# Four modulation rows summed in other places, and a softmax with its sink among the scores

## Chip, cores and metric

One core of a Trainium2 chip. The metric is the device time of one execution in microseconds; lower is better. TensorE's clock has two levels, 1.2 and 2.4 GHz; the profile gives the granted share of the higher one.

## The reference, cut to what matters

One transformer layer on 1024 latent tokens of width 1024 with 256 context tokens: a modulated norm, eight heads of windowed attention beside a short convolution, an output projection, then a mixture of 16 experts.

```python
mod = silu(c) @ w_ada + b_ada                # (1024) @ (1024, 6*1024)
sh1, sc1, gt1, sh2, sc2, gt2 = split(mod, 6)
h = modulate(rmsnorm(x, g_mix), sh1, sc1)    # r*(1+scale)+shift
q, k, v, bg, cg, hv = split(h @ w_in)
att = windowed_attention(rope(q), rope(k), v, k_ctx, v_ctx, sink)
#   p = softmax([sink, q.k_ctx/8, q.k_loc/8]); the sink's share is dropped
conv = bg * conv3(cg * hv)
x = x + gt1 * (concat(att, conv) @ w_out)
h2 = modulate(rmsnorm(x, g_ffn), sh2, sc2)
x = x + gt2 * expert_choice_ffn(h2, w_router, w_gate, w_up, w_down)
return rmsnorm(x, g_final)
```

The text calls gt1, sh2, sc2 and gt2 the rows 0 to 3. `sh1` and `sc1` are computed first, on TensorE, and stay as they are.

## The kernel before

All products that need fp32 accuracy are made of three fp32r products: each operand is split into a rounded high part (ScalarE) and a low part, source minus high (VectorE or GpSimd).

The order of TensorE's instructions is as written. Those of the other engines, and of the SP queue that issues loads, are put in order by a planner from a time model, by readiness and priority; each engine then runs its own list in order. `weave` mixes streams: each stream yields weights, and the stream that has done the smallest share of its total goes on.

*Projections.* `kv_stream` runs over 24 steps: eight 128-column groups of the 256 context tokens, then of the first and of the second 512 latent tokens. A step calls `build_hT` (transposes on TensorE, scale and shift, high part, low part; even and odd groups on different engines, L290 to L298) and three steps later `proj_kv`. `q_stream` follows, one tile of 128 tokens after the other: 24 matmuls, rotation and split on VectorE and ScalarE (L506 to L511), then, inside the next tile, eight transposes (`q_turn`). It also turns the late keys. The key/value weights are split at L264 to L269, their low part on GpSimd.

Beside these runs `mod_stream`, woven from 18 of 56 parts on. For each of the rows 0 to 3 and each of eight 128-row groups of `w_ada` it loads 128x1024 numbers (L461), ScalarE multiplies them by silu(c) of the partition (L462) and GpSimd adds them to the row's accumulator (L464). TensorE sums each accumulator over the partitions by a selection matrix (L474), `b_ada` is added, and the four rows go to memory (`rows_d`).

*Attention and convolution* are woven next. A unit is a pair of heads of one 128-token tile, 32 in all. `scores` makes the scores in PSUM; VectorE adds the mask and takes the maximum with 8 times the sink (L576); L578 scales it to the exponential's bias; ScalarE takes the exponential and its sum (L579); L586 to L589 add exp(sink - maximum) to the sum and invert it. Both heads are then scaled, and `values` transposes, splits and multiplies them. The score buffers are two slots in turn. `conv` loads a weight block one part ahead (12 parts) and GpSimd makes its low part (L712). `router_consts` (L650) reads rows 1 and 2 back in transposed form.

*Output projection.* For each tile 48 matmuls (L879), the residual on VectorE (L884), the norm, and beside it routing and sorting of earlier tiles (L1001 to L1067), nearly all on VectorE. The split tokens `ah` rotate through three free slots. Experts' weights are prefetched into the other slots.

The last uses are: row 0 at L777, rows 1 and 2 at L831 to L835 and in `router_consts`, row 3 in the experts.

Of the kernel before, what the change touches and what calls it, by code (L numbers as in the profile page):

```python
# [86 lines left out]
def tile_layer(ctx, tc, x, c, cx, c_ctx, w_ada, b_ada, g_mix, w_in, conv_w, sink, w_out, g_ffn,  # L87
# [59 lines left out]
    nc.sync.dma_start(small[8:16], c_ctx.rearrange("(k p) -> k p", p=128))  # L147
    nc.sync.dma_start(small[16:32], b_ada[:, 0:2 * D].rearrange("o (k p) -> (o k) p", p=128))
    nc.sync.dma_start(small[32:40], g_mix.rearrange("o (k p) -> (o k) p", p=128))
    nc.sync.dma_start(small[40:52], conv_w.rearrange("o t (f p) -> (o t f) p", p=128))  # L150

# [15 lines left out]
    nc.vector.memset(ones_b, 1.0)  # L167
    sel = consts.tile([128, 4, 4], F32, name="sel")
    nc.vector.memset(sel, 0.0)
    for r in range(4):  # L170
        nc.vector.memset(sel[:, r, r:r + 1], 1.0)

    smallT = consts.tile([128, 52], F32, name="smallT")
    ps = p1n("ps_small")
    nc.tensor.transpose(ps[:, :52], small[:52], ident[:52, :52])
    nc.vector.tensor_copy(smallT, ps[:, :52])
    gmixT = smallT[:, 32:40]
    convT_w = smallT[:, 40:52]

# [96 lines left out]
    nc.sync.dma_start(sinkb, sink.partition_broadcast(128).rearrange("p o h -> p (o h)"))  # L276
    nc.vector.tensor_scalar(sink8, sinkb, 8.0, None, op0=OP.mult)

# [3 lines left out]
    def build_hT(tiles, j, hT, k, mem=None):  # L282

        n = 128 * len(tiles)
        ps = p1n("ps_xt", 3)
        for i, t in enumerate(tiles):
            nc.tensor.transpose(ps[:, i * 128:(i + 1) * 128], t[:, k * 128:(k + 1) * 128], ident)
        hf = mem[:, k % 4] if mem is not None else w4("hf", (n,), tag=("w4", "wm")[k % 2])
        hi, lo = hT[2 * (k // 4)][0][:, k % 4], hT[2 * (k // 4) + 1][0][:, k % 4]
        if k % 2:  # L290
            nc.scalar.activation(hf, ps[:, :n], AF.Identity, scale=mscale[:, k, j:j + 1], bias=mshift[:, k, j:j + 1])
            nc.vector.tensor_copy(hi, hf)
            nc.vector.tensor_tensor(lo, hf, hi.bitcast(F32), op=OP.subtract)
        else:
            nc.vector.tensor_scalar(hf, ps[:, :n], mscale[:, k, j:j + 1], mshift[:, k, j:j + 1],
                                    op0=OP.mult, op1=OP.add)
            nc.scalar.copy(hi, hf)
            (nc.gpsimd if mem is None or k < 4 else nc.vector).tensor_tensor(lo, hf, hi.bitcast(F32), op=OP.subtract)  # L298

# [154 lines left out]

    mrows = p2(0, "mrows")

    def mod_row(r, acc):

        for k in range(KC):
            wt = wm("wmod")  # L460
            nc.sync.dma_start(wt, wada_k[k][:, (2 + r) * D:(3 + r) * D])  # L461
            nc.scalar.activation(wt if k else acc, wt, AF.Copy, scale=silu_c[:, k:k + 1])  # L462
            if k:
                nc.gpsimd.tensor_tensor(acc, acc, wt, op=OP.add)  # L464
            yield 1

    def mod_stream():
        yield 18
        accs = []

        def sums(j):
            for r in (2 * j, 2 * j + 1):
                for n in range(2):
                    mm(mrows[:4, n], sel[:, r], accs[j][0][:, r % 2, n * 512:(n + 1) * 512], start=r == 0, stop=r == 3)  # L474
            slots.put(accs[j][1])

        for j in range(2):
            accs.append(slots.get((2, D), F32, "acc"))
            g = [mod_row(2 * j + i, accs[j][0][:, i]) for i in range(2)]
            for k in range(KC):  # L480
                for q in g:
                    yield next(q)
                if j == 1 and k == 2:
                    sums(0)
        bias = w4("bias")
        nc.sync.dma_start(bias[0:4], b_ada[:, 2 * D:6 * D].rearrange("o (r f) -> (o r) f", r=4))
        yield 3
        yield 3
        sums(1)
        nc.vector.tensor_tensor(bias[0:4], mrows[:4].rearrange("p a b -> p (a b)"), bias[0:4], op=OP.add)  # L490
        nc.sync.dma_start(rows_d, bias[0:4])

# [42 lines left out]

    weave([(urgent(steps(kv_stream(), q_stream())), 95.0), (mod_stream(), 56.0)])
    for r in wq:
# [14 lines left out]
    def scores(u):  # L552
# [4 lines left out]
        loc = slice(blocks[0] * 128, (blocks[-1] + 1) * 128)  # L557
        sm2, s_sm = slots.get((2, 640), F32, "sm")
        for i in range(2):
# [14 lines left out]
            else:  # L574
                mk = maskt[:, 0:W]
            nc.vector.tensor_tensor_reduce(dst, src, mk, op0=OP.add, op1=OP.max, scale=1.0,  # L576
                                           scalar=sink8[:, h:h + 1], accum_out=mx[:, b, h:h + 1])
# [7 lines left out]
        r = rec[:, b, hs]  # L585
# [14 lines left out]
    def values(u):  # L600
# [49 lines left out]
    def router_consts():  # L650
# [7 lines left out]
        nc.sync.dma_start(wr, w_router.rearrange("o (k p) e -> p (o k) e", p=128))  # L658
        modT = work.tile([24, 128], F32, tag="sa", name="modT")
        for i, src in enumerate((rows_d[1], rows_d[2], g_ffn[0])):  # L660
            nc.sync.dma_start(modT[8 * i:8 * i + 8], src.rearrange("(k p) -> k p", p=128))
        yield
        pmod = p1(2, "pmod")
        nc.tensor.transpose(pmod[:, :24], modT, ident[:24, :24])
        b2T = consts.tile([128, KC], F32, name="b2T")
        s2T = consts.tile([128, KC], F32, name="s2T")
        nc.vector.tensor_copy(s2T, pmod[:, 16:24])
        nc.vector.tensor_copy(b2T, pmod[:, 0:8])
        nc.vector.scalar_tensor_tensor(s2T, pmod[:, 8:16], 1.0, s2T, op0=OP.add, op1=OP.mult)
        yield  # L670
# [144 lines left out]

    weave([(steps(attention(), prepare()), 160.0), (conv(), 161.0)])

# [14 lines left out]
    bcast_row(S2, rows_d[2])  # L832
    gf = wm("gf")
    bcast_row(gf, g_ffn[0])
    nc.vector.scalar_tensor_tensor(S2, S2, 1.0, gf, op0=OP.add, op1=OP.mult)  # L835

# [308 lines left out]
    def beside(t, others):  # L1145
# [323 lines left out]
def _constants():  # L1469
# [10 lines left out]
    amask = np.zeros((128, 768), np.float32)  # L1480
    amask[:, 256:384] = np.where(j >= q, 0.0, NEG)
    amask[:, 512:640] = np.where(j <= q, 0.0, NEG)
    amask = amask.astype(ml_dtypes.bfloat16)
# [33 lines left out]
```

## Time and profile before

| | us |
|---|---|
| median of 3 runs (1166.91 to 1170.52) | 1169.38 |
| the profiled execution | 1168.05 |
| its span, first to last instruction | 1166.3 |
| TensorE busy | 1061.0 (91%) |
| VectorE busy | 966.0 (83%) |
| ScalarE busy | 765.4 (66%) |
| GpSimd busy | 353.3 (30%) |
| mean granted TensorE clock | 0.961 |

The span is what the trace covers; the rest of an execution lies around it. Busy shares are means over stages with different limits, so the rows below go by stretches. A busy TensorE may still run at half its clock, and the time of an instruction on VectorE or GpSimd includes the time in which it is held.

### The profile page before, as it was taken

The page shows a single profiled execution, that of the slowest core. Times are in us where ns is not written, and L with a number is a line of the kernel's source. Part 1 is how long each engine was busy: PE and PEld are TensorE (multiplying, and loading weights), DVE is VectorE, ACT ScalarE, POOL GpSimd, SP SyncE. Part 2 cuts the span into 40 slices and gives each one's busy share as a digit, 9 for nine tenths or more (in the row PEclk, how much of TensorE's full clock was granted, in tenths as well). Part 3 has the DMA queues.
Part 4 walks back from the last instruction along what each step waited for, and adds up shares of the span by engine and source line. Part 5 has one row for each costly group of instructions (what it writes and reads, how often), then busy time and mean ns, then how long its engine had stood idle before and what let it go on. Part 6 is the DMA issues. An engine that isn't in the chain of part 4 may idle for free.

```text
span 1166.3 us, 15621 instructions
## 1 busy us (share of the span) xinstructions
PE 1061.0 (91%) x5486; PEld 875.6 (75%) x5486; DVE 966.0 (83%) x1661; ACT 765.4 (66%) x1057; POOL 353.3 (30%) x294
## 2 busy tenths in 40 slices
PE   6787889999899998998299999999999999999982
PEld 2675667888788877887188888888888888888861
DVE  7787455887878785489889999999999999999975
ACT  7566655766666743222178788778788778888853
POOL 0457681312203131221303333313333312330022
PEclk9797999999999998999599999999999999999996
DMA  9644540100101188657589999999999999999555
GB/s 375 231 163 144 164 145 20 37 19 1 55 1 37 31 307 293 163 142 267 225 295 353 410 393 390 391 390 387 407 394 387 390 391 386 403 398 391 219 182 233
DMA packets 90502, 291.84 MB, mean 250 GB/s; under 512 B 7012, under 2 KB 20784, under 8 KB 89400
## 3 DMA queue, kind: packets, MB, share of 16 engines
q1 hardware_dynamic: 84808, 270.40, 60.7%
q0 software_dynamic: 5616, 20.45, 7.2%
q8 instruction: 43, 0.70, 0.2%
q14 instruction: 35, 0.29, 0.1%
HBM read 266.69 MB, written 24.13 MB: 249 GB/s over the span
## 4 chain that ended last, share of the span: by engine, by line
PE 71%; DVE 11%; DMA 7%; ACT 4%; issue 4%; POOL 2%; POOLq 0%; ACTq 0%; DVEq 0%; SPq 0%
PE pg L1284 14%; PE pu L1284 14%; PE py L1284 13%; PE po L879 6%; PE ps_cv L732 3%; PE ps_cv L731 3%; PE ps_cv L733 3%; PE pt L623 2%; PE po_att L614 2%; DMA xt<-in_x_dram 2%; PE ps_s L566 2%; PE xTp L1270 1%; DVE whl L1133 1%; PE ps_s L564 1%; PE hTtp L1270 1%
## 5 line engine op out<-in xcount | busy, mean ns | idle before, releaser
L1133 DVE TENSOR_TENSOR whl<-raw,whl 128x1024 fp32r<-128x1024 f32 x384 | 455.2, 1224 | 30.5 <-ACT whl L1130 19.6
L1130 ACT CAST whl<-raw 128x1024 fp32r<-128x1024 f32 x384 | 400.2, 1054 | 101.1 <-PE pu L1284 35.7
L1284 PE MATMUL pg<-whl,xT 128*128 128x512 f32 x768 | 187.1, 396 | 2.1 <-DVE whl L1133 2.1
L1284 PE MATMUL pu<-whl,xT 128*128 128x512 f32 x768 | 180.9, 392 | 0.0
L1284 PEld LDWEIGHTS pg<-whl,xT 128*128 128x128 f32 x768 | 142.9, 189 | 31.9 <-DVE whl L1133 2.9
L1284 PE MATMUL py<-whl,hTt 128*128 128x512 f32 x720 | 165.8, 389 | 0.0
L1284 PEld LDWEIGHTS pu<-whl,xT 128*128 128x128 f32 x768 | 143.0, 188 | 29.5
L1284 PEld LDWEIGHTS py<-whl,hTt 128*128 128x128 f32 x720 | 135.1, 188 | 28.4 <-DVE whl L1133 0.3
L1249 POOL TENSOR_SCALAR oh<-iota,pos 128x128 bf16<-128x128 f32 x108 | 106.7, 1002 | 13.3 <-DVE pos L1234 12.8
L1342 POOL DMA_INDIRECT acc_d<-yt,idx x15 | 38.4, 2560 | 195.9 <-DVE yt L1330 195.9
L731 PE MATMUL ps_cv<-hTh,wcs 128*128 128x512 f32 x192 | 81.6, 425 | 0.0
L1294 POOL DMA_INDIRECT xr<-h_d,idx x16 | 21.7, 1357 | 188.8 <-DVE gate_w L1260 188.8
L464 POOL TENSOR_TENSOR acc<-acc,wmod 128x1024 f32<-128x1024 f32 x28 | 69.4, 2494 | 26.4 <-ACT wmod L462 25.9
L626 ACT CAST pth<-pt 128x512 fp32r<-128x512 f32 (+1 forms) x88 | 46.1, 524 | 46.3 <-PE pt L623 46.2
L733 PE MATMUL ps_cv<-hTh,wcs 128*128 128x512 f32 x192 | 76.3, 397 | 0.0
L732 PE MATMUL ps_cv<-hTl,wcs 128*128 128x512 f32 x192 | 76.2, 397 | 0.0
L879 PE MATMUL po<-woh,ah 128*128 128x512 f32 x240 | 71.3, 407 | 0.6 <-ACT woh L224 0.6
L627 DVE TENSOR_TENSOR pth<-pt,pth 128x512 fp32r<-128x512 f32 (+1 forms) x88 | 53.9, 613 | 20.1 <-ACT pth L626 19.2
L712 POOL TENSOR_TENSOR wcs<-wcr,wcs 128x1024 fp32r<-128x1024 f32 x12 | 28.6, 2389 | 110.0 <-ACT wcs L711 87.4
L579 ACT ACTIVATE sm<-sm,negm 128x640 f32<-128x640 f32 (+1 forms) x64 | 51.6, 807 | 4.4 <-DVE negm L578 4.3
L576 DVE CUSTOM_DVE_ANT_0 sm<-ps_s,maskt,sink 128x640 f32<-128x640 f32 (+1 forms) x56 | 48.3, 863 | 6.9 <-PE ps_s L566 6.3
L879 PEld LDWEIGHTS po<-woh,ah 128*128 128x128 f32 x240 | 44.6, 193 | 9.5 <-ACT woh L224 1.0
(285 smaller groups left out, 1821.6 us busy)
## 6 DMA issues: line engine op xcount, KB each, us to landing
raw<-in_w_gate_dram SPq DMA_DIRECT2D x64, 1024.0 KB, 10.1
raw<-in_w_up_dram SPq DMA_DIRECT2D x64, 1024.0 KB, 8.1
raw<-in_w_down_dram SPq DMA_DIRECT2D x64, 1024.0 KB, 10.4
wmod<-in_w_ada_dram SPq DMA_DIRECT2D x32, 512.0 KB, 3.8
wa<-in_w_ada_dram SPq DMA_DIRECT2D x8, 1024.0 KB, 9.5
wcr<-in_w_in_dram SPq DMA_DIRECT2D x12, 512.0 KB, 4.2
xt<-in_x_dram SPq DMA_DIRECT2D x4, 1024.0 KB
wor<-in_w_out_dram SPq DMA_DIRECT2D x4, 1024.0 KB
```

What stands on the lines that cost most here:

```text
L464: nc.gpsimd.tensor_tensor(acc, acc, wt, op=OP.add)
L576: nc.vector.tensor_tensor_reduce(dst, src, mk, op0=OP.add, op1=OP.max, scale=1.0, scalar=sink8[:, h:h + 1], accum_out=mx[:, b, h:h + 1])
L579: nc.scalar.activation(sm, sm, AF.Exp, bias=negm[:, b, h:h + 1], scale=0.125, accum_out=esum[:, b, h:h + 1])
L627: nc.vector.tensor_tensor(pth[:, 1, :n], pt[:, :n], pth[:, 0, :n].bitcast(F32), op=OP.subtract)
L731: mm(ps, wsp[:, 0, k], hi, start=k == 0, stop=False)
L732: mm(ps, wsp[:, 0, k], lo, start=False, stop=False)
L733: mm(ps, wsp[:, 1, k], hi, start=False, stop=k == KC - 1)
L879: mm(po[n], a, wo[k // 4, n][j][:, k % 4], start=first, stop=last)
L1130: nc.scalar.copy(w[:, 0], t[:, k % 2])
L1133: low = nc.vector.tensor_tensor(w[:, 1], t[:, k % 2], w[:, 0].bitcast(F32), op=OP.subtract)
L1249: nc.gpsimd.tensor_scalar(oh[:, t], iota1, pos[:, t, 0, e:e + 1], None, op0=OP.is_equal)
L1284: mm(ps[n], a_hl[:, a, k], w[:, j, n * 512:(n + 1) * 512], start=first, stop=last)
```

## The change

It does five things.

1. Rows 1 and 2 alone are summed beside the projections, from 14 of 34 parts on. VectorE multiplies and adds in one instruction (`mod_add`); TensorE sums each 128 columns by a product with a column of ones, which gives the row in transposed form (`mod_sums`), with `b_ada`, and `1 + scale` times `g_ffn` for row 2; `mod_row` turns it and stores it.
2. Row 0 is summed in attention, in column blocks of 384, 384 and 256, its accumulator in PSUM beside the values' product; row 3 in the output projection beside tiles 1 to 4.
3. The sink is a column of the scores, written by GpSimd; queries are scaled by -1/8, the mask's sign is turned, the maximum becomes a minimum, and the exponential has scale -1. L578 and L586 to L588 go.
4. `build_hT` uses ScalarE for scale, shift and high part and VectorE for the low part in every step; the low part of the key/value weights moves from GpSimd to VectorE.
5. `b_ada` and `g_ffn` are loaded in transposed form at the start; their later loads and products go.

```diff
-    nc.sync.dma_start(small[16:32], b_ada[:, 0:2 * D]...)
+    nc.sync.dma_start(small[16:64], b_ada.rearrange("o (k p) -> (o k) p", p=128))
...
+    nc.sync.dma_start(small[84:92], g_ffn.rearrange("o (k p) -> (o k) p", p=128))
...
-        nc.gpsimd.tensor_tensor(wkv_l[:, ks], wkv_r[:, ks], wkv_h[:, ks].bitcast(F32), op=OP.subtract)
+        nc.vector.tensor_tensor(wkv_l[:, ks], wkv_r[:, ks], wkv_h[:, ks].bitcast(F32), op=OP.subtract)
...
-        if k % 2:
-            ... ScalarE scale and shift, VectorE high and low
-        else:
-            ... VectorE scale and shift, ScalarE high, GpSimd or VectorE low
+        nc.scalar.activation(hf, ps[:, :n], AF.Identity, scale=mscale[:, k, j:j + 1], bias=mshift[:, k, j:j + 1])
+        nc.scalar.copy(hi, hf)
+        nc.vector.tensor_tensor(lo, hf, hi.bitcast(F32), op=OP.subtract)
...
+    def mod_add(src, k, acc, out=None):
+        if k == 0:
+            nc.vector.tensor_scalar(acc, src, silu_c[:, 0:1], None, op0=OP.mult)
+        else:
+            nc.vector.scalar_tensor_tensor(acc if out is None else out, src, silu_c[:, k:k + 1], acc,
+                                           op0=OP.mult, op1=OP.add)
+    def mod_sums(pr, acc, r, k0=0):
+        n = acc.shape[1] // 128
+        for q in range(n):
+            mm(pr[:, q:q + 1], acc[:, q * 128:(q + 1) * 128], ones_f, start=True, stop=True)
+        c = 8 * r + k0
+        v = modv[:, c:c + n]
+        nc.vector.tensor_tensor(v, pr[:, 0:n], badaT[:, c:c + n], op=OP.add)
+        if r == 2:
+            nc.vector.scalar_tensor_tensor(v, v, 1.0, gffnT[:, k0:k0 + n], op0=OP.add, op1=OP.mult)
+    def mod_row(pr, r):
+        nc.tensor.transpose(pr[:8, :128], modv[:, 8 * r:8 * r + 8], ident)
+        row = w4("prow", (128,))
+        nc.scalar.copy(row[:8], pr[:8, :128])
+        nc.sync.dma_start(rows_d[r].rearrange("(k p) -> k p", p=128), row[:8])
...
+    def mod_stream():
+        yield 14
+        acc, s_acc = slots.get((2, D), F32, "acc")
+        items = [(k, r) for k in range(KC) for r in (1, 2)]
+        for i in range(len(items) + 2):
+            ... load of item i, mod_add of item i - 2
+            yield 1
+        yield 1
+        pr = p2(0, "prow")
+        for r in (1, 2):
+            mod_sums(pr[:, r - 1], acc[:, r - 1], r)
+        for r in (1, 2):
+            mod_row(pr[:, r - 1], r)
+    def mod_attention(accp):
+        stage = work.tile([128, 2, 384], F32, tag="early", name="stage")
+        cols = (slice(0, 384), slice(384, 768), slice(768, 1024))
+        items = [(n, k) for n in range(3) for k in range(KC)]
+        ... two loads ahead
+        yield 4
+        for i, (n, k) in enumerate(items):
+            ...
+            mod_add(src, k, accp[:, :w], src if last else None)
+            if last:
+                yield 1
+                mod_sums(accp, src, 0, cols[n].start // 128)
+            load(i + 2)
+            yield 1
+        mod_row(p1(3, "prow"), 0)
...
-        nc.scalar.copy(qs[:, :, 0, :], tv)
-        nc.vector.tensor_tensor(qs[:, :, 1, :], tv, qs[:, :, 0, :].bitcast(F32), op=OP.subtract)
+        nc.scalar.activation(qs[:, :, 0, :], tv, AF.Copy, scale=-0.125)
+        nc.vector.scalar_tensor_tensor(qs[:, :, 1, :], tv, -0.125, qs[:, :, 0, :].bitcast(F32), op0=OP.mult,
+                                       op1=OP.subtract)
...
-    weave([(urgent(steps(kv_stream(), q_stream())), 95.0), (mod_stream(), 56.0)])
+    weave([(urgent(steps(kv_stream(), q_stream())), 95.0), (mod_stream(), 34.0)])
...
-        sm2, s_sm = slots.get((2, 640), F32, "sm")
+        sm2, s_sm = slots.get((2, 648), F32, "sm")
+        nc.gpsimd.tensor_copy(sm2[:, :, W], sink8[:, 2 * hp:2 * hp + 2])
...
-            nc.vector.tensor_scalar(negm[:, b, h:h + 1], mx[:, b, h:h + 1], -0.125, None, op0=OP.mult)
-            nc.scalar.activation(sm, sm, AF.Exp, bias=negm[:, b, h:h + 1], scale=0.125,
+            sx = sm2[:, i, :W + 1]
+            nc.scalar.activation(sx, sx, AF.Exp, bias=mx[:, b, h:h + 1], scale=-1.0,
                                  accum_out=esum[:, b, h:h + 1])
...
-        nc.vector.tensor_tensor(r, sinkb[:, hs], negm[:, b, hs], op=OP.add)
-        nc.scalar.activation(r, r, AF.Exp)
-        nc.vector.tensor_tensor(r, r, esum[:, b, hs], op=OP.add)
-        nc.vector.reciprocal(r, r)
+        nc.vector.reciprocal(rec[:, b, hs], esum[:, b, hs])
...
-    weave([(steps(attention(), prepare()), 160.0), (conv(), 161.0)])
+    weave([(steps(attention(), prepare()), 160.0), (conv(), 161.0), (mod_attention(pb[:, 1]), 45.0)])
...
-    nc.vector.scalar_tensor_tensor(S2, S2, 1.0, gf, op0=OP.add, op1=OP.mult)
...
+    def last_row():
+        mem, s_ = slots.get((4, 512), F32, "gt2")
+        ... 16 loads of 128x512, three ahead; yield 6
+        for i, (n, k) in enumerate(items):
+            mod_add(mem[:, 1 + i % 3], k, mem[:, 0])
+            load(i + 3)
+            if k == KC - 1:
+                yield 1
+                mod_sums(p1(1, "prow"), mem[:, 0], 3, 4 * n)
+            yield 1.8
+        mod_row(p1(1, "prow"), 3)
...
     for t in range(NT - 1):
-        beside(t, [[0.0, before(t)]])
+        lr = [[0.0, last_row_part()]] if 1 <= t < 5 else []
+        beside(t, [[0.0, before(t)]] + lr)
```

## Rows read from the trace of the kernel before

**Rows 1.** Stretches: length, busy us PE, PEld, DVE, ACT, POOL; clock; DMA share, GB/s

```profile
36.00:45.00 9.00, 7.45 (x41) 6.43 (x41) 5.59 (x18) 8.51 (x17) 3.37 (x5) 0.69 0.67 237
45.00:92.40 47.40, 40.30 (x283) 37.33 (x283) 37.57 (x48) 29.04 (x44) 23.55 (x15) 0.90 0.43 144
92.40:177.20 84.80, 67.00 (x298) 49.66 (x297) 52.80 (x78) 46.75 (x65) 62.43 (x39) 0.94 0.49 156
177.20:430.00 252.80, 245.63 (x1455) 211.37 (x1456) 195.61 (x508) 164.94 (x345) 54.42 (x23) 0.99 0.15 49
442.00:550.00 108.00, 106.76 (x574) 90.99 (x574) 72.14 (x321) 31.27 (x73) 24.37 (x49) 0.97 0.67 208
```

**Rows 2.** Timeline of 14 to 37 us: start, length, instruction

```profile
30.64 5.08 POOL L269 TENSOR_TENSOR wkvl<-wkvr,wkvh 128x1024 fp32r<-128x1024 f32 x2 [0.88 <-ACT wkvh L268]
31.38 2.08 DVE L255 TENSOR_TENSOR pmTv<-mparts 128x32 f32<-128x32 f32 x1
33.50 2.24 DVE L260 TENSOR_TENSOR mshift<-pmTv,smallT 128x8 f32<-128x8 f32 x1
```

**Rows 3.** Groups by line, 0 to 400 us: count, busy us, mean ns, idle before

```profile
L396 DVE TENSOR_TENSOR wql<-wqr,wqh 128x1024 fp32r<-128x1024 f32 x4 | 5.0, 1302 | 0.9 <-ACT wqh L395 0.9
L291 ACT ACTIVATE hf<-ps_xt,mshift,mscale 128x512 f32<-128x512 f32 x4 | 3.1, 774 | 0.0
L291 ACT ACTIVATE hf<-ps_xt,mshift,mscale 128x256 f32<-128x256 f32 x4 | 2.2, 556 | 4.6 <-DVE mscale L262 4.6
L297 ACT CAST hcTh<-hf 128x256 fp32r<-128x256 f32 x4 | 1.6, 394 | 1.6 <-DVE hf L295 1.6
L578 DVE TENSOR_SCALAR negm<-mx 128x1 f32<-128x1 f32 x61 | 9.3, 152 | 1.9
```

**Rows 4.** Single lines of the whole span: ns min/median/max, first and last start

```profile
L354 DVE TENSOR_TENSOR kp<-t,kp x4: 684/2433/2880, 98.0 to 113.6; 128x512 fp32r<-128x512 f32 x4
L588 DVE TENSOR_TENSOR rec<-rec,esum x32: 142/160/2326, 184.7 to 408.5; 128x2 f32<-128x2 f32 x32
L627 DVE TENSOR_TENSOR pth<-pt,pth x88: 402/690/693, 188.9 to 415.0; 128x512 fp32r<-128x512 f32 x64, 128x256 fp32r<-128x256 f32 x24
L674 PE MATMUL pbias<-wr,b2T x16: 178/262/263, 337.2 to 338.8; 128*128 128x16 f32 x16
L935 DVE SCALAR_TENSOR_TENSOR h<-xres,rstd,rowsA x6: 1283/1284/1287, 453.4 to 521.9; 128x1024 f32<-128x1024 f32 x6
```

**Rows 5.** TensorE's timeline, 62 to 125 us, first transposes of two steps

```profile
66.46 0.60 PE L287 MATMUL ps_xt<-ident,xt 128*128 128x128 f32 x4
...
72.06 0.60 PE L287 MATMUL ps_xt<-ident,xt 128*128 128x128 f32 x4
```

**Rows 6.** The chain that ended last, 30 to 185 us: start, length, what

```profile
119.38 0.23 PE ps_q L502
...
123.51 0.87 PE pq L521 x8
...
138.55 3.53 PE mrows L474 x8
```

**Rows 7.** Waits of TensorE, 36 to 180 us: total, times, longest

```profile
PE pq L521 <- DVE qs L511: 12.4, 5, 4.6
```

**Rows 8.** Waits, 176 to 440 us: total, times, longest

```profile
POOL wcs L712 <- ACT wcs L711: 85.0, 8, 20.8
...
PE po_att L614 <- DVE pth L627: 4.9, 8, 1.1
```

**Rows 9.** Stretches of the output projection and the sort, columns as in Rows 1

```profile
454.00:488.00 34.00, 34.00 (x183) 29.11 (x182) 9.53 (x22) 6.90 (x17) 9.61 (x20) 1.00 0.66 176
488.00:520.00 32.00, 32.00 (x168) 27.15 (x167) 27.70 (x142) 10.14 (x25) 7.25 (x14) 1.00 0.42 108
...
550.00:570.00 20.00, 2.35 (x18) 1.59 (x18) 18.06 (x105) 4.95 (x10) 2.40 (x9) 0.59 0.76 294
```

**Rows 10.** The page's loads: count, KB each, median us to landing

```profile
wmod<-in_w_ada_dram SPq DMA_DIRECT2D x32, 512.0 KB, 3.8
```

More of the change, by code (lines that the diff above doesn't have):

```diff
@@ L147, in tile_layer @@
     nc.sync.dma_start(small[8:16], c_ctx.rearrange("(k p) -> k p", p=128))
-    nc.sync.dma_start(small[16:32], b_ada[:, 0:2 * D].rearrange("o (k p) -> (o k) p", p=128))
-    nc.sync.dma_start(small[32:40], g_mix.rearrange("o (k p) -> (o k) p", p=128))
-    nc.sync.dma_start(small[40:52], conv_w.rearrange("o t (f p) -> (o t f) p", p=128))
+    nc.sync.dma_start(small[16:64], b_ada.rearrange("o (k p) -> (o k) p", p=128))
+    nc.sync.dma_start(small[64:72], g_mix.rearrange("o (k p) -> (o k) p", p=128))
+    nc.sync.dma_start(small[72:84], conv_w.rearrange("o t (f p) -> (o t f) p", p=128))
+    nc.sync.dma_start(small[84:92], g_ffn.rearrange("o (k p) -> (o k) p", p=128))
     for k in range(1, KC):
@@ L167, in tile_layer @@
     nc.vector.memset(ones_b, 1.0)
[L168 to L173, printed above, removed]
-    ps = p1n("ps_small")
[L175 to L178, printed above, removed]
+    ones_f = consts.tile([128, 1], F32, name="ones_f")
+    nc.vector.memset(ones_f, 1.0)
+    smallT = consts.tile([128, 92], F32, name="smallT")
+    ps = p1n("ps_small")
+    nc.tensor.transpose(ps[:, :92], small[:92], ident[:92, :92])
+    nc.vector.tensor_copy(smallT, ps[:, :92])
+    badaT = smallT[:, 32:64]
+    gmixT = smallT[:, 64:72]
+    convT_w = smallT[:, 72:84]
+    gffnT = smallT[:, 84:92]
     silu_c = consts.tile([128, 16], F32, name="silu_c")
@@ L452, in tile_layer @@
     nc.sync.dma_start(maskt, amask)
[L455 to L464, printed above, removed]
-            yield 1
[L467 to L491, printed above, removed]
@@ new lines, in tile_layer @@
+    modv = consts.tile([128, 32], F32, name="modv")
+    def mod_add(src, k, acc, out=None):
+        if k == 0:
+            nc.vector.tensor_scalar(acc, src, silu_c[:, 0:1], None, op0=OP.mult)
+        else:
+            nc.vector.scalar_tensor_tensor(acc if out is None else out, src, silu_c[:, k:k + 1], acc, op0=OP.mult,
+                                           op1=OP.add)
+    def mod_sums(pr, acc, r, k0=0):
[7 more added lines that the diff above has]
+            nc.vector.scalar_tensor_tensor(v, v, 1.0, gffnT[:, k0:k0 + n], op0=OP.add, op1=OP.mult)
@@ new lines, in mod_row, with mod_load @@
+    def mod_row(pr, r):
[3 more added lines that the diff above has]
+        nc.sync.dma_start(rows_d[r].rearrange("(k p) -> k p", p=128), row[:8])
+    def mod_load(dst, r, k, cols):
+        nc.sync.dma_start(dst, wada_k[k][:, (2 + r) * D + cols.start:(2 + r) * D + cols.stop])
+    def mod_stream():
+        yield 14
+        acc, s_acc = slots.get((2, D), F32, "acc")
+        items = [(k, r) for k in range(KC) for r in (1, 2)]
+        st_, mem = {}, []
+        for i in range(len(items) + 2):
+            if i == 8:
+                mem.append(slots.get((2, D), F32, "acc"))
+            if i < len(items):
+                k, r = items[i]
+                st_[i] = wm("wmod") if not mem or i % 3 == 2 else mem[0][0][:, i % 3]
+                mod_load(st_[i], r, k, slice(0, D))
+            if i > 1:
+                k, r = items[i - 2]
+                mod_add(st_.pop(i - 2), k, acc[:, r - 1])
+            yield 1
+        slots.put(mem[0][1])
+        yield 1
+        pr = p2(0, "prow")
+        for r in (1, 2):
+            mod_sums(pr[:, r - 1], acc[:, r - 1], r)
+        slots.put(s_acc)
+        for r in (1, 2):
+            mod_row(pr[:, r - 1], r)
@@ new lines, in mod_attention, with load @@
+    def mod_attention(accp):
+        stage = work.tile([128, 2, 384], F32, tag="early", name="stage")
+        cols = (slice(0, 384), slice(384, 768), slice(768, 1024))
+        items = [(n, k) for n in range(3) for k in range(KC)]
+        def load(i):
+            if i < len(items):
+                n, k = items[i]
+                w = cols[n].stop - cols[n].start
+                mod_load(stage[:, i % 2, :w], 0, k, cols[n])
+        load(0)
+        load(1)
+        yield 4
+        for i, (n, k) in enumerate(items):
+            w = cols[n].stop - cols[n].start
+            src = stage[:, i % 2, :w]
+            last = k == KC - 1
+            mod_add(src, k, accp[:, :w], src if last else None)
[5 more added lines that the diff above has]
+        mod_row(p1(3, "prow"), 0)
@@ L658, in router_consts @@
         nc.sync.dma_start(wr, w_router.rearrange("o (k p) e -> p (o k) e", p=128))
[L659 to L669, printed above, removed]
+        b2T, s2T = modv[:, 8:16], modv[:, 16:24]
         yield
@@ L1156, in beside, with load @@
                 pass
+    def last_row():
+        mem, s_ = slots.get((4, 512), F32, "gt2")
+        items = [(n, k) for n in range(2) for k in range(KC)]
+        def load(i):
+            if i < len(items):
+                n, k = items[i]
+                mod_load(mem[:, 1 + i % 3], 3, k, slice(n * 512, n * 512 + 512))
+        for i in range(3):
+            load(i)
+        yield 6
+        for i, (n, k) in enumerate(items):
[6 more added lines that the diff above has]
+        mod_row(p1(1, "prow"), 3)
+        slots.put(s_)
+        while True:
+            yield 99
+    lrow = last_row()
     def before(t):
@@ L1163, in before, with last_row_part @@
         return steps(*side)
+    def last_row_part():
+        c = 0.0
+        while c < 10:
+            w = next(lrow)
+            c += w
+            yield w
     def once(f, *args):
@@ L1480, in _constants @@
     amask = np.zeros((128, 768), np.float32)
-    amask[:, 256:384] = np.where(j >= q, 0.0, NEG)
-    amask[:, 512:640] = np.where(j <= q, 0.0, NEG)
+    amask[:, 256:384] = np.where(j >= q, 0.0, -NEG)
+    amask[:, 512:640] = np.where(j <= q, 0.0, -NEG)
     amask = amask.astype(ml_dtypes.bfloat16)
```

18 lines of the change are left out of this document (4 added, 14 removed).

## The prediction

> **What bounds the kernel now.** I read the stretches first [rows 1]. They are the context tokens (36 to 45 us), the key/value projection of the latent tokens (to 92.4), the query projection (to 177.2), attention beside the convolution (to 430), and the output projection with routing (442 to 550). Behind these stand the experts, which the change doesn't touch. TensorE is busy 245.6 of 252.8 us in attention and 106.8 of 108 in the output projection, so little can be won there. It is busy only 40.3 of 47.4 and 67.0 of 84.8 in the two projections, and those are the stretches in which GpSimd works hardest: 23.6 and 62.4 us [rows 1].
>
> Then I read what single VectorE instructions cost there. The same subtraction L354 takes 0.68 us at best and 2.43 in the median [rows 4]; the one at L255, on 32 elements, takes 2.08, beside a GpSimd subtraction of the same moment [rows 2]. So VectorE isn't short of time: it is held while GpSimd runs a tensor-tensor. The waits say who pays: TensorE waits 12.4 us in five places for the query rows that VectorE splits [rows 7].
>
> The profiled execution took 1168.05 us, 1.75 more than its span; the median of the runs is 1169.38, 1.3 above it. I sum against 1168.05 and add 1.3.
>
> **Start (30 to 36 us).** The key/value weights' low parts move from GpSimd (5.08 us) to VectorE. L255 and L260 should fall from 2.08 and 2.24 (two instructions) to about 0.15 each, as another small one takes (L578, 0.152 [rows 3]), which is 3.9 us off a chain on which nothing else runs [rows 2]. Against that stand two subtractions of the shape of L396, 1.30 us each [rows 3]; they are ready before the scale and shift, and may go ahead of them. Bounds -3.9 to -1.3; I take **-2.6**, the middle, since either order can come out.
>
> **Context (36 to 45).** Every modulated column group now goes through ScalarE twice (scale and shift, then rounding); before, each of the four even ones had only its rounding there and each odd one only its scale. That adds four of 0.556 and four of 0.394, 3.8 us [rows 3], to an engine that is busy 8.5 of these 9 us [rows 1]. It also squares the eight latent tiles here, and the next stretch waits for the first four. Bounds 0 to +3.8; I take **+2**.
>
> **Key/value projection (45 to 92.4).** One step takes TensorE 5.60/3 = 1.87 us where nothing holds it [rows 5]. Sixteen make 29.9; three left-over context steps of half the size 2.8; eight transposes 0.87 [rows 6]: 33.6. The other 13.8 us are waiting and a clock below full (0.90 in the mean [rows 1]). After the change GpSimd has no tensor-tensor here, since the modulation rows start only when 14 of 34 parts of the weave are done, which is where the key/value steps end. ScalarE then carries scale and rounding of every step, at most twice 0.77 = 1.55 us [rows 3] of TensorE's 1.87, besides the rounding of weights and keys: it becomes the second limit. Bounds -13.8 to -3; I take 5 of the 13.8 as staying: **-8.8**.
>
> **Query projection (92.4 to 177.2).** TensorE's own work: 18 matmuls between 119.38 and 123.51, so 0.229 each, 192 of them 44.0; 64 query transposes 8 x 0.87 = 7.0; 32 key transposes 3.5; two column sums of 3.53 [rows 6]: 61.6 of 84.8. The sums go (-7.1). In their place come 16 small fp32 products; eight of the nearest kind took 1.7 us (L674, 16 records from 337.2 to 338.8 at their starts [rows 4]), so 3.4. Then one chain that nothing covers, since the code gives no step between sums and turn: sum, add of b_ada, factor, transpose, copy, before the scores may use the same bank; I estimate 2 us. The modulation rows leave ScalarE and GpSimd. Sixteen VectorE instructions of the size of L935 (1.28 us [rows 4]) come instead, 20.5 us, beside rotations and splits that fall back to their minimum. They are queued with the query chain, which is given priority, so one can be in the way at most each time: on average half of 1.28, eight times, 5 us (bounds 0 and the 12.4 of now). I leave 3 for the first tile, which needs a bank that the keys are still read from, and 3 for the clock. 54.5 + 3.4 + 2 + 5 + 3 + 3 = 71: **-13.8**, bounds -25 to -4.
>
> **Attention.** From VectorE go 64 scalings (0.15) and 64 instructions of the running denominator; half of these, L588, take 0.16 in the median but up to 2.33 when GpSimd reads [rows 3, 4]. That shortens the softmax chain of each unit by three hops. TensorE waited for its end product only 4.9 us in all [rows 8], so at most about 5 us is to be had. Added are 24 partial sums for row 0. Their accumulator lies in PSUM; L627 (512 wide, one input in PSUM) never took over 0.693 us though GpSimd works here too [rows 4], so 384 columns are some 0.52 and 256 some 0.40: 11.5 us on VectorE, less than what goes (64 x 0.152 and 32 x 0.16 alone are 14.8). That is what the Trainium skill says too (SBUF — State Buffer, "Who interferes with whom"): only instructions with two SBUF inputs, or in a two-port mode, are held by a GpSimd read. Were they held as L588 is, each could cost up to 2.33, 56 us in all on VectorE; the row decides for the first. On SP 24 loads stand between those of the convolution's weights, each waiting for one of two buffers; a weight load goes out one part (252.8/12 = 21 us) ahead, so I cost them at nothing; uncovered, each late one holds about a load, 3.8 us [rows 10]. TensorE gets eight more products, +1.7. Sum **-1** (bounds -5 to +10; the upper end is the GpSimd write, third rival).
>
> **Output projection and the sorting behind it.** Row 3 adds eight products (+1.7) and 16 VectorE instructions of 512 columns, half of L935, 0.64 each. Half of them fall in tiles 1 and 2, where VectorE is free (9.5 of 34 us); the rest meet a VectorE that is busy 27.7 of 32 and 18.1 of 20 to the end of the sort [rows 9]. Up to 8 x 0.64 = 5.1 of that can come out at the end, and the second group of products waits in TensorE's order for the last add. The slot that row 3 borrows leaves two for the split tokens, still one ahead. Bounds 0 to +9; I take **+3.5**. Loads, the one dropped product of g_ffn and the moved constants I cost at nothing: the loads ride on a queue whose DMA share is 0.15 to 0.67 in these stretches [rows 1].
>
> **Sum.** -2.6 + 2 - 8.8 - 13.8 - 1 + 3.5 = -20.7: 1147.4 profiled, 1148.7 as a run.
>
> **Rivals.** *The whole gap closes.* If TensorE sets the pace of both projections, the key/value stretch falls by 12.6 instead of 8.8 and the query stretch to 60 (54.5, the products and their chain), by 24.8: 14.8 more, **1134**. For it: GpSimd leaves both. Against it: ScalarE's 1.55 us a step beside its other work. The Trainium skill (Trainium Kernel Development and Optimization, "Performance Expectations") would judge by weight loads rather than by matmul busy time. They fill 49.7 of 84.8 us here against 211.4 of 252.8 in attention [rows 1]; at that density the query stretch would last 59 us, so by that rule this rival is right for it.
>
> *The adds take the place of the port.* If the planner sets two adds of 1.28 into each of the eight query chains, 20 us come back, 15 more than I allow: **1164**, still faster; at the half, 1156. For it: the adds wait in order for loads of 3.8 us [rows 10], and VectorE then stands for all. Against it: each load is issued two steps ahead.
>
> *Slower: GpSimd stands in the softmax.* Each of 32 units now needs GpSimd to write the sink columns before the exponential. GpSimd runs in order and already sits up to 20.8 us behind a ScalarE cast (85 us in eight waits [rows 8]). Where a write is planned behind such a subtraction, the exponential, the next transposes and TensorE wait. From 0.65 us held per unit (20.7/32) the gain is gone; at half of such a subtraction, 5.08/2/2 = 1.27 us [rows 2], 41 us come on top: **1189**. For it: the 20.8. Against it: the planner sees the cast coming and the write is ready a unit earlier.
>
> *Nothing moves*: the waits of the projections are set by something else, such as the loads; DMA share is 0.43 and 0.49 there [rows 1], so I give it little: 1169.
>
> **Chances.** Forecast (1139 to 1157) 0.5, whole gap (1130 to 1139) 0.19, adds in the way (1157 to 1166) 0.16, slower 0.09, nothing 0.06. A difference under 0.3% (3.5 us) can't be told from none here. So faster 0.85, same 0.06, slower 0.09. The range, 1131 to 1164, holds the forecast, most of the whole-gap case and most of the third; the forecast's own is 1139 to 1157.
>
> **What would show it.** Right: in the profile after, L255, L354 and the rotation stand at their minimum, the first scores start near 154 us instead of 177, and attention keeps its length of some 253 us. Wrong at the adds: TensorE's wait for the split query rows stays near 12 us. Wrong in attention: an exponential that waits for a GpSimd copy. Wrong in the tail: the sort ends over 3 us later, counted from the start of the output projection, than now.

## The result, and the profile after

The kernel after takes **1177.33 us** (median of nine runs, 1175.13 to 1184.2) against 1168.83 of the kernel before in the same session: ratio 1.0083, 95% interval 1.0064 to 1.0102. It is slower, by 0.8%. The forecast was 1148.7 with a range of 1131 to 1164, so sign and range are both wrong. The profiled execution, the fastest of the nine, took 1175.13 us with a span of 1173.4; before, the span was 1166.3. So the stretches below account for some 7 of the 8.5 us between the medians.

The stretches of after that answer to [rows 1], with the same columns; their ends are the same events (first query product, first scores, end of attention):

```profile
36.00:45.00 9.00, 6.78 (x36) 5.87 (x36) 2.44 (x12) 9.00 (x21) 1.21 (x2) 0.64 0.87 295
45.00:86.60 41.60, 36.81 (x287) 35.32 (x288) 26.02 (x41) 31.80 (x55) 1.20 (x2) 0.96 0.31 99
86.60:165.10 78.50, 61.09 (x316) 50.98 (x314) 47.02 (x92) 22.85 (x44) 5.22 (x4) 0.92 0.29 101
165.10:437.00 271.90, 256.94 (x1472) 218.10 (x1473) 186.39 (x406) 159.40 (x314) 63.71 (x67) 0.97 0.19 59
449.00:559.00 110.00, 108.14 (x591) 91.85 (x591) 80.96 (x337) 31.08 (x74) 25.86 (x49) 0.99 0.74 237
```

GpSimd left both projections as planned (5.22 us instead of 62.43 in the query stretch), and in the query stretch VectorE and ScalarE are lighter too. Yet the query stretch is only 6.3 us shorter, and attention is 19 us longer. Between matmuls of the same place, in the two profiled spans:

| stretch | before | after | difference | forecast |
|---|---|---|---|---|
| to the first context scale (L291) | 36.15 | 35.88 | -0.3 | -2.6 |
| from there to the first query product | 56.2 | 50.7 | -5.5 | -6.8 |
| first query product to first scores | 84.8 | 78.6 | -6.2 | -13.8 |
| first to last scores | 227.9 | 246.5 | +18.6 | -1 with the next row |
| last scores to first output product | 27.2 | 27.6 | +0.4 | |
| output projection and sort | 148.7 | 150.8 | +2.1 | +3.5 |
| experts | 585.3 | 583.4 | -1.9 | not in the sum |

The sum is +7.2. The context and key/value stretches together and the output projection behaved about as costed; the start gave 0.3 instead of 2.6 us. The two large misses are the query stretch and attention, and the trace shows both. Each time is of one profiled execution: runs 5 and 9 below leave everything up to the first scores as it is in after, and their query stretches took 79.7 and 78.5 us, so a difference of some 1 us says nothing.

**The query stretch.** TensorE's waits from 86 to 166 us of after (total, times, longest; compare [rows 7]):

```profile
PE pq L565 <- DVE qs L554: 10.2, 1, 10.2
PE ps_q L544 <- DVE t L325: 3.3, 1, 3.3
PE pk L366 <- DVE kp L349: 1.7, 1, 1.7
```

Five waits have become one; the prediction had named a wait that stays near 12 us as the sign that the sums are in the way. Its VectorE timeline (start, length, instruction) and two stretches:

```profile
105.27 0.68 DVE L323 TENSOR_TENSOR t<-ps_q,ropet 128x512 f32<-128x512 f32 x1
105.87 0.68 DVE L325 TENSOR_TENSOR t<-ps_q,ropet 128x512 f32<-128x512 f32 x1
106.46 1.27 DVE L458 SCALAR_TENSOR_TENSOR acc<-wmod,silu_c,acc 128x1024 f32<-128x1024 f32 x1
...
108.06 1.27 DVE L458 SCALAR_TENSOR_TENSOR acc<-acc,silu_c,acc 128x1024 f32<-128x1024 f32 x1
109.26 0.41 DVE L329 TENSOR_TENSOR t<-t 128x256 f32<-128x256 f32 x1
109.59 0.41 DVE L330 TENSOR_TENSOR t<-t 128x256 f32<-128x256 f32 x1
109.94 1.28 DVE L458 SCALAR_TENSOR_TENSOR acc<-acc,silu_c,acc 128x1024 f32<-128x1024 f32 x1
...
112.94 0.68 DVE L554 SCALAR_TENSOR_TENSOR qs<-t,qs 128x512 fp32r<-128x512 f32 x1
...
```
```profile
100.00:120.00 20.00, 8.25 (x42) 7.04 (x43) 16.80 (x29) 5.22 (x12) 0.00 (x0) 0.74 0.51 164
120.00:155.00 35.00, 35.00 (x176) 29.37 (x175) 14.44 (x27) 10.22 (x19) 0.00 (x0) 1.00 0.00 1
```

The sums (L458) take 1.27 to 1.28 us each; nothing holds them. But all sixteen run between 83 and 116 us, and one of them stands at nearly every hop of the first query tile's chain. TensorE is busy 8.25 of 20 us there and the granted clock falls to 0.74; afterwards it runs 35 us without a gap beside a VectorE that is 41% busy.

**Attention.** The third scaling of after with what surrounds it (other rows left out), and the same place of before:

```profile
185.85 2.36 POOL L742 TENSOR_TENSOR wcs<-wcr,wcs 128x1024 fp32r<-128x1024 f32 x1 [0.91 <-ACT wcs L741]
...
186.52 0.17 DVE L629 RECIPROCAL rec<-esum 128x2 f32<-128x2 f32 x1 [1.62 <-ACT sm L624]
186.72 1.77 DVE L635 TENSOR_SCALAR sm<-sm,rec 128x512 f32<-128x512 f32 x1
...
188.41 0.68 DVE L667 TENSOR_TENSOR pth<-pt,pth 128x512 fp32r<-128x512 f32 x1
...
189.15 0.65 PE L654 MATMUL po_att<-pth,vx 128*128 128x256 f32 x2 [1.63 <-DVE pth L667]
```
```profile
197.75 2.40 POOL L712 TENSOR_TENSOR wcs<-wcr,wcs 128x1024 fp32r<-128x1024 f32 x1 [20.77 <-ACT wcs L711]
...
198.13 0.69 DVE L627 TENSOR_TENSOR pth<-pt,pth 128x512 fp32r<-128x512 f32 x1 [1.13 <-ACT pth L626]
...
198.88 0.50 PE L614 MATMUL po_att<-pth,vx 128*128 128x256 f32 x2 [0.22 <-DVE pth L627]
198.94 1.23 DVE L588 TENSOR_TENSOR rec<-rec,esum 128x2 f32<-128x2 f32 x1
```

The reader is to see one GpSimd subtraction meeting two orders. Before, the longer softmax chain came to its held instruction (L588, 1.23 us) only after VectorE had made the last low half that TensorE needed: no low half waited for it, and TensorE's next wait, for the scaled scores at 200.94 us, was 0.39 us. After, the chain is three hops shorter, so the reciprocal and the scaling L635 come up first; L635 is held until GpSimd is done (1.77 instead of 0.49 us), and the low half L667, which this unit's products need, waits behind it. TensorE needs the scaled scores only in the next unit. Of TensorE's waits for its end product, the first line below (after, 165 to 412 us; compare [rows 8]), five are over 1 us (1.17 to 1.68), and each has a held L635 right ahead of the low half:

```profile
PE po_att L654 <- DVE pth L667: 8.5, 7, 1.7
PE po_att L654 <- ACT pth L666: 1.5, 4, 0.5
```

Before was not free of this: five of its waits, 0.56 to 1.45 us long, stand behind a held instruction of the denominator (L586 or L588). The exponential of after waits for the minimum, not for the sink copy (ScalarE, same columns):

```profile
ACT sm L624 <- DVE mx L621: 26.6, 26, 3.1
```

These waits are not the whole of the 18.6 us. Between first and last scores TensorE's idle time grew from 6.0 to 13.4 us. And at three of the five waits over 1 us the granted clock fell to the lower level, 1.2 GHz, for about 3.4 us (columns as in [rows 1]):

```profile
189.30:192.80 3.50, 3.50 (x14) 3.10 (x15) 1.86 (x5) 0.37 (x1) 0.00 (x0) 0.51 0.02 5
315.60:319.00 3.40, 3.40 (x13) 3.00 (x13) 1.94 (x6) 0.37 (x1) 0.00 (x0) 0.50 0.53 152
380.50:383.90 3.40, 3.17 (x11) 2.98 (x12) 1.93 (x8) 0.37 (x1) 0.00 (x0) 0.50 0.00 0
```

Before, it stayed at 1.00 from 182 us to the last scores. By an estimate from these rows, three times 3.4 us at half the clock cost some 5 us. The other 6 us, among them the products of row 0, were not taken apart.

### The profile page after: what moved, and what is told of

Its sections match the earlier page's. It is cut to its first block, busy times and chain, and to the rows that moved or that the text cites. A ratio compares the mean times of both kernels' runs of the same rounds, so it can differ in the third digit from the quotient of the medians.

```text
span 1173.4 us, 15673 instructions
## 1 busy us (share of the span) xinstructions
PE 1063.7 (91%) x5537; PEld 881.6 (75%) x5537; DVE 944.0 (80%) x1576; ACT 739.4 (63%) x1021; POOL 277.1 (24%) x286
## 4 chain that ended last, share of the span: by engine, by line
PE 73%; DVE 11%; issue 5%; DMA 5%; ACT 4%; POOL 1%; POOLq 0%; DVEq 0%; ACTq 0%; SPq 0%
PE pg L1348 15%; PE pu L1348 14%; PE py L1348 13%; PE po L907 4%; PE po_att L654 3%; PE ps_cv L761 3%; PE ps_cv L762 3%; PE ps_cv L763 3%; PE pt L663 2%; DMA gt<-in_w_ada_dram 2%; PE ps_s L611 2%; PE xTp L1334 1%; PE ps_s L609 1%; PE hTtp L1334 1%; DVE sm L635 1%
## 5 line engine op out<-in xcount | busy, mean ns | idle before, releaser
L1313 POOL TENSOR_SCALAR oh<-iota,pos 128x128 bf16<-128x128 f32 x108 | 106.6, 1001 | 13.4 <-PE pf L1296 12.8
L624 ACT ACTIVATE sm<-sm,mx 128x641 f32<-128x641 f32 (+1 forms) x64 | 51.7, 808 | 26.7 <-DVE mx L621 26.6
L667 DVE TENSOR_TENSOR pth<-pt,pth 128x512 fp32r<-128x512 f32 (+1 forms) x88 | 52.4, 611 | 12.7 <-ACT pth L666 12.5
L663 PEld LDWEIGHTS pt<-ident,sm 128*128 128x128 f32 x304 | 39.0, 143 | 14.0 <-issue 2.6
```

The source lines that it names most:

```text
L624: nc.scalar.activation(sx, sx, AF.Exp, bias=mx[:, b, h:h + 1], scale=-1.0, accum_out=esum[:, b, h:h + 1])
L663: nc.tensor.transpose(pt[:, (2 * q + i) * 128:(2 * q + i + 1) * 128], sm2[:, i, j * 128:(j + 1) * 128], ident)
L667: nc.vector.tensor_tensor(pth[:, 1, :n], pt[:, :n], pth[:, 0, :n].bitcast(F32), op=OP.subtract)
L1313: nc.gpsimd.tensor_scalar(oh[:, t], iota1, pos[:, t, 0, e:e + 1], None, op0=OP.is_equal)
```

## The experiments

Times between first and last scores go from the first to the last scores matmul (227.9 before, 246.5 after). The first four expectations, written earlier, count to the last unit's first matmul, which gives 2.4 us less (225.5 and 244.1). All ratios are to the kernel before on the same chip, with their 95% intervals. Stage times are again of one profiled execution each.

**1. Without the sums of row 0.**

```
-  (loads, 24 mod_add, mod_sums of mod_attention)
+  yield 31
+  nc.vector.memset(modv[:, 0:8], 0.0)
```

> The kernel after, without the summing of modulation row 0 during attention (24 loads, 24 VectorE sums and 8 products are left out and zeros stand for the row; what reads the row stays). First scores to last scores lasted 225.5 us before and 244.1 after. Theory A, the sums of row 0 in VectorE's queue are what attention lost: this run shows 225 to 230 and some 1160 us. Theory B, the shortened softmax moved the scaling of the scores (L635) to where GpSimd's reads hold it, whatever the sums do: 240 to 244 and 1174 to 1177 us.

Measured: 1169.79 us, ratio 0.9992 (0.9983 to 1.0002); scores 237.5 us. Between the theories: the sums cost 9.0 of the 18.6, not all. L635 is still held up to 1.78 us. The whole time counts for less here: with zeros for the row the later data differ, and the output projection and sort took 153.8 us instead of 150.8.

**2. The softmax of before in the kernel after.**

```
-  nc.gpsimd.tensor_copy(sm2[:, :, W], sink8[...])        # and the minimum, -1/8
+  r = rec[:, b, hs]                                       # L586 to L589 of before
+  nc.vector.tensor_tensor(r, sinkb[:, hs], mx[:, b, hs], op=OP.add)
...
```

> The kernel after, with the softmax of before (maximum, its scaling, the chain for the denominator; no sink column, queries not scaled); the sums of row 0 stay. Theory A (the sums): first to last scores stay at 240 to 250 us, 1174 to 1182 us in all. Theory B (the shortened softmax): 225 to 230 and some 1160 us.

Measured: 1172.16 us, 1.0017 (1.0005 to 1.0029); 240.8 us. The new softmax costs 5.7 us here; again neither theory alone.

**3. The convolution's low parts on VectorE.**

```
-  nc.gpsimd.tensor_tensor(wsp[:, 1], raw, wsp[:, 0].bitcast(F32), op=OP.subtract)
+  nc.vector.tensor_tensor(wsp[:, 1], raw, wsp[:, 0].bitcast(F32), op=OP.subtract)
```

> The kernel after, with the low parts of the twelve convolution weights (L742, 2.4 us each on GpSimd) subtracted on VectorE, some 1.1 to 1.3 us each, 15 us in all. Theory B, GpSimd's reads hold the scaling L635: the holds beside L742 go, L635 stays under 0.7 us but for those beside L791, and about half of the lost 18.6 us comes back (232 to 238 us, 1166 to 1172 us). Theory A (VectorE's queue is too full of row-0 sums): 15 us more on VectorE make it no better, 244 us or more, 1177 to 1184.

Measured: 1174.2 us, 1.0033 (1.0021 to 1.0044); 242.4 us. It got better (by 4.1 us) although VectorE got the twelve subtractions on top; it points to the holds, at less than half the gain that I expected. No scaling is held beside the low parts any more, as expected; five still take 0.80 to 2.51 us, four beside the sums of the taps (L791) and one, which I had not foreseen, beside L786.

**4. The new softmax alone, in the kernel before.**

```
-  r = rec[:, b, hs]                                       # L586 to L589, and L578
+  nc.gpsimd.tensor_copy(sm2[:, :, W], sink8[:, 2 * hp:2 * hp + 2])
+  nc.vector.reciprocal(rec[:, b, hs], esum[:, b, hs])     # minimum and -1/8 as in the change
```

> The kernel before, with the new softmax alone (sink as a column, minimum, queries times -1/8); modulation rows as before. Theory A: attention keeps 222 to 227 us between first and last scores, 1165 to 1169 us in all. Theory B: 240 to 244 and 1183 to 1188 us.

Measured: 1178.82 us, 1.0063 (1.0046 to 1.0079); 235.4 us. So the softmax costs 7.5 us without any of the sums: theory A falls as the only cause. The query stretch grew too, from 84.8 to 91.0 us; GpSimd still adds rows there, and TensorE's wait for the split query rows was 14.3 instead of 12.4 us. The rest of that was not followed up.

**5. Both scalings on ScalarE.**

```
-            if i:
-                nc.scalar.activation(sm2[:, i, :W], sm2[:, i, :W], AF.Copy, scale=share)
-            else:
-                nc.vector.tensor_scalar(sm2[:, i, :W], sm2[:, i, :W], share, None, op0=OP.mult)
+            nc.scalar.activation(sm2[:, i, :W], sm2[:, i, :W], AF.Copy, scale=share)
```

> The kernel after, with both scalings of the softmax on ScalarE (L635, 0.49 to 2.51 us on VectorE, becomes an activation of 0.84). Theory B, what the new softmax costs attention (5.7 to 7.5 us by the runs so far) comes from L635 standing ahead of the low halves in VectorE's queue and being held there by GpSimd: without it, first to last scores go from 246.5 to 238 to 241 us, 1169 to 1172 us in all, and the steady units from 7.08 to 6.95 us. Rival C, the cost is the new chain's other steps (sink copy, exponential before the low half): 246 or more and 1177 or more, as ScalarE gets 9 us of work on top.

Measured: 1163.46 us, 0.9934 (0.9907 to 0.9961); 232.9 us, 13.6 us back, more than expected. The waits of 165 to 412 us above, in this run (167 to 401 us):

```profile
PE po_att L651 <- ACT pth L663: 2.4, 4, 1.1
PE po_att L651 <- DVE pth L664: 0.6, 3, 0.2
```

The 8.5 us for VectorE's low half have become 0.6, and from 171 us to the last scores the granted clock stays at 1.00. Rival C falls. This one line turns the change from slower into faster than before. The run takes away both L635's place and its hold; run 9 parts them.

**6. The sums of rows 1 and 2 paced by the query tiles.**

```
-            mod_add(st_.pop(i - 2), k, acc[:, r - 1])
+            while g is not None and g not in gates:
+                yield 0.3
+            mod_add(src, k, acc[:, r - 1], None, sg[:, g, c:c + 1])   # first six: silu_c
...
+        nc.vector.scalar_tensor_tensor(sg[:, t, 0:n], qs[:, 0, 1, 0:n].bitcast(F32), 0.0,
+                                       silu_c[:, cols], op0=OP.mult, op1=OP.add)
+        gates.add(t)
```

> The kernel after, with the sums of rows 1 and 2 spread over the query tiles: six of the sixteen before the first tile, then two per tile, each made to read a factor that is written only after that tile's split rows (one tiny VectorE instruction per tile); products during the last tile. Theory D, the bunch of sums at 83 to 115 us holds the first tile's chain (TensorE's single wait of 10.2 us): the query stage falls from 78.6 to 67 to 71 us and the run to 1166 to 1170. Rival E, the wait is for the keys' and values' processing, which stands in the same queue whatever the sums do: 76 to 79 us and 1175 to 1178.

Measured: 1154.7 us, 0.9856 (0.9827 to 0.9884); query stretch **60.6 us**, 18 less than after and below what I expected. The stretch, and TensorE's wait in it:

```profile
86.00:146.70 60.70, 59.19 (x316) 50.16 (x316) 41.40 (x89) 21.98 (x42) 3.65 (x3) 0.97 0.25 79
```
```profile
PE pq L583 <- DVE qs L567: 1.3, 1, 1.3
```

From the first product of the first query tile to that of the third it takes 16.8 us instead of 33.0; from the start of the last tile to the scores 12.1 instead of 13.7. The later tiles take 6.4 us in both. So the bunch ahead of the first tile was nearly the whole loss, and rival E falls: the keys' processing stands in the same queue here. How it is ordered now (VectorE, the second tile):

```profile
103.44 0.42 DVE L330 TENSOR_TENSOR t<-t 128x256 f32<-128x256 f32 x1
104.62 0.69 DVE L567 SCALAR_TENSOR_TENSOR qs<-t,qs 128x512 fp32r<-128x512 f32 x1 [0.76 <-ACT qs L566]
105.35 0.16 DVE L573 SCALAR_TENSOR_TENSOR sg<-qs,silu_c 128x2 f32<-128x2 f32 x1
105.55 2.48 DVE L461 SCALAR_TENSOR_TENSOR acc<-wmod,sg,acc 128x1024 f32<-128x1024 f32 x2
109.44 0.69 DVE L323 TENSOR_TENSOR t<-ps_q,ropet 128x512 f32<-128x512 f32 x1 [1.41 <-PE ps_q L558]
```

**7. Rows 0 to 2 early, the softmax of before.** Row 0 is summed in PSUM with a third sum per tile; `mod_attention` is gone; of the context steps, the rounding goes to VectorE:

```
+        (nc.vector.tensor_copy if n == 256 else nc.scalar.copy)(hi, hf)
+            items.append((0, t, t, 0))
-    weave([..., (mod_attention(pb[:, 1]), 45.0)])
```

> Rows 0, 1 and 2 summed beside the query projection in the spread manner (three sums per tile, row 0 in PSUM), nothing of it in attention; softmax of before; rounding of the eight context steps on VectorE instead of ScalarE; the rest as after. If the losses are the sums in attention (9 us) and the new softmax (6 to 7), attention returns to 227 to 230 us; with a query stage of 67 to 72 and a first latent step 1 to 3 us earlier, 1144 to 1152 us. If the spread sums still hold the chains, the query stage stays at 78 or more and the run at 1155 to 1160.

Measured: **1144.15 us, 0.9770 (0.9742 to 0.9799)**; it beats both kernels. Query stretch 70.4 (as expected), scores 226.0 (1 better than expected), first query product at 82.0 us instead of 86.6, of which the sixth run (86.0, without that edit) says that 4 belong to the rounding.

**8. The same with the new softmax, both scalings on ScalarE.**

```
+            nc.scalar.activation(sm2[:, i, :W], sm2[:, i, :W], AF.Copy, scale=share)
```

> As the run with rows 0 to 2 summed early, but with the new softmax and both its scalings on ScalarE. Theory B: attention as good as with the softmax of before, or up to 3 us better since the chain is three hops shorter, 226 to 230 us, 1142 to 1152 in all. Rival C: 234 us or more, 1150 to 1158.

Measured: 1146.82 us, 0.9788 (0.9760 to 0.9816); scores 224.9, 3.0 below before but only 1.1 below run 7, which differs from it in the softmax and its scalings alone. So with its scalings on ScalarE the shorter chain no longer costs anything; that it gains is not shown, and as a whole the run is no faster than run 7. Its experts took 4.3 us longer than those of run 7 in the two profiled executions (run 10's took as long as its own); why stays open.

**9. No two-input GpSimd instructions in attention.**

```
-        nc.gpsimd.tensor_tensor(wsp[:, 1], raw, wsp[:, 0].bitcast(F32), op=OP.subtract)
-                    nc.gpsimd.tensor_tensor(y, y, tap, op=OP.add)
```

> The kernel after, with GpSimd's two-input instructions of attention left out: the twelve low parts of the convolution weights (the third product reads the high part instead) and the eight sums of the convolution's taps. The scaling L635 stays on VectorE in its place in the queue. If the holds by GpSimd are the cost that moving the scalings to ScalarE took away, L635 stays at 0.49 to 0.58 us throughout (but beside the four L786 that are left) and first to last scores go from 246.5 to 231 to 236 us. If its place ahead of the low halves costs by itself, 238 to 243 us.

Measured: 235.3 us between the scores, 11.2 back (the whole run, 1161.06 us, counts for less, since later data differ). L635 of after, and of this run (ns min/median/max, first and last start):

```profile
L635 DVE TENSOR_SCALAR sm<-sm,rec x31: 486/554/2506, 172.7 to 407.7; 128x640 f32<-128x640 f32 x24, 128x512 f32<-128x512 f32 x7
```
```profile
L635 DVE TENSOR_SCALAR sm<-sm,rec x31: 486/553/991, 172.2 to 396.5; 128x640 f32<-128x640 f32 x24, 128x512 f32<-128x512 f32 x7
```

L635 stands where it stood, TensorE's wait for VectorE's low half fell from 8.5 to 2.9 us, and the granted clock stays at 1.00 from 168 us to the last scores. By the profile no other engine waits for GpSimd in this stretch of after, so I put what came back down to the holds and not to GpSimd's own work. The place alone is worth, by this comparison, some 2.4 us, what is left to run 5, which itself put more work on ScalarE.

**10. Twelve sums early, two per tile.**

```
+        items = [(r, k, None, 0) for k in range(6) for r in (1, 2)]
...
```

> As the run with rows 0 to 2 summed early and both scalings on ScalarE, with twelve sums instead of six before the first query tile (beside the key/value steps, where VectorE is busy about half the time) and two per tile instead of three. If three sums per tile is what kept its query stage at 70.5 us (7.3 us a tile instead of 6.4), this one takes 61 to 64, key/value steps no later by more than 2 us, 1133 to 1141 us in all. If the twelve delay the key/value steps, the first query product comes 3 us or more later and nothing is won: 1144 to 1148.

Measured: 1144.16 us, 0.9762 (0.9735 to 0.9790). Query stretch 64.6, 5.9 less than run 8; but the first query product comes at 88.3 instead of 82.2. TensorE's wait (36 to 88 us; in run 8 it is 2.2, once) and VectorE's timeline say why:

```profile
PE ps_kv L314 <- DVE hTl L293: 6.8, 3, 3.6
```
```profile
76.98 1.28 DVE L461 SCALAR_TENSOR_TENSOR acc<-wmod,silu_c,acc 128x1024 f32<-128x1024 f32 x1 [1.72 <-DMA wmod<-in_w_ada_dram]
78.18 0.69 DVE L293 TENSOR_TENSOR hTl<-hfs,hTh 128x512 fp32r<-128x512 f32 x1
...
82.91 1.22 DVE L391 TENSOR_TENSOR wql<-wqr,wqh 128x1024 fp32r<-128x1024 f32 x1
84.05 1.28 DVE L461 SCALAR_TENSOR_TENSOR acc<-wmod,silu_c,acc 128x1024 f32<-128x1024 f32 x1
85.24 0.69 DVE L293 TENSOR_TENSOR hTl<-hfs,hTh 128x512 fp32r<-128x512 f32 x1
```

A sum at the head of the queue waits 1.72 us for its load, and the key/value step behind it waits along; that cost TensorE 1.0 us. The longest wait, 3.6 us up to 85.98, is no wait for a load: sums and weight subtractions (L391) in turn stand ahead of one low half. The second reading held.

## Why the prediction was wrong, step by step

- *Start (-2.6).* -0.3. L255 and L260 fell to 0.18 and 0.16 as said, but both low parts of the key/value weights (1.22 us each) went ahead of the scale and shift, and the context's normalisation came first. The bound of -1.3 that I gave for that order was itself too good.
- *Context and key/value (+2 and -8.8).* -5.5 together against -6.8. Mechanism and size were about right: ScalarE is busy 9.00 of 9 us where it was 8.51, and run 7 shows what its eight context roundings cost, some 4 us by comparison with run 6.
- *Query projection (-13.8, bounds -25 to -4).* -6.2. The TensorE work of 54.5 + 3.4 was right: run 6 does the stretch in 60.6, the first rival's 60. (My estimate by the Trainium skill, Trainium Kernel Development and Optimization, "Performance Expectations", which judges by weight loads, had been 59; the trace of run 6 agrees, with 50.16 us of weight loads in 60.70.) The step that failed is "one can be in the way at most each time": I spread the sums evenly over eight tiles because the code yields evenly. They bunched instead, all sixteen between 83 and 116 us, and the first tile's chain waited for them. The rival "adds take the place of the port" had the right mechanism and put it in eight places; it was one, with a falling clock behind it.
- *Attention (-1, bounds -5 to +10).* +18.6, and the failing step is "That shortens the softmax chain of each unit by three hops", with "at most about 5 us" to be had. I costed what leaves VectorE and did not ask where the remaining instructions would stand, though one L595 of 1.06 us beside GpSimd's L756 stood in the trace of before. The new softmax alone made the stage 7.5 us longer (run 4); without GpSimd's two-input instructions 11.2 us came back (run 9), with the scaling off VectorE 13.6 (run 5). The first has the gain of the shorter chain in it, and in the last two the sums of row 0 stand in the same queue; how these add up was not taken apart. (The Trainium skill, SBUF — State Buffer, "Who interferes with whom", names both kinds: two SBUF inputs, and a scaling in a two-port mode, which GpSimd blocks for its whole instruction. The trace agrees for L588, held up to 2.33 us, and for L635, up to 2.51, beside two-input GpSimd instructions; beside L786 the hold ended earlier, as said below. I had applied it to the new sums alone, which at 0.62 us were indeed not held.)
- *Sums of row 0 ("less than what goes").* I had put them at 11.5 us on VectorE and at nothing in the sum. They took 13.7 us there and cost 9.0 (run 1), 8.0 with the scalings on ScalarE (runs 5 and 8). Only some of that is seen in single waits: 0.6 before a group of products. The rest, among it the clock (0.97 in this stretch, 0.98 in run 1), was not taken apart.
- *Third rival (GpSimd stands in the softmax).* Right sign and stretch, wrong place: the exponential waits for the minimum (26.6 us), never for the sink copy; what GpSimd delayed was the scaling.
- *Output projection (+3.5).* +2.1. Fourteen of the sixteen sums took 0.75 instead of 0.64 us.

The chances failed with the mechanism: 0.09 for slower, given to a single place, was too little for an edit that reorders a queue shared with GpSimd.

## What to carry to other kernels

Taking hops out of a chain can move its last instructions forward in every queue they stand in: ask what they now pass, and whether that instruction can be held. Work "beside" a stage that has no dependency on the stage need not spread over it: here it bunched in front of the first consumer, and a data dependency (a 0.16 us instruction per tile) spread it. If one of two VectorE instructions is exposed to GpSimd's reads, let the exposed one be the one nobody waits for, or put it on ScalarE.

## What the hardware showed that I had not expected

A held scaling waits for the end of the whole GpSimd instruction where that has two inputs: in after, seven of them issued 0.24 to 1.28 us into one of 2.4 us and ended 0.28 to 0.36 us behind its end. Beside L786, a GpSimd scaling with one tensor input that took 2.87 us, L635 took 0.99 us and ended 1.40 us before it; why is not shown. A low half with one input in PSUM passes the same GpSimd instruction in its usual 0.69 us.
